# Output projection: two weight tiles in turns over the column chunks, and some element-wise work moved from VectorE to GpSimd

## The chip, the cores and the metric

The kernel runs on one core of a Trainium2 chip. The metric is the device time of one execution in microseconds (us); several runs were made, and their median counts. The engines are TensorE (PE, with weight loads shown apart as PEld), VectorE (DVE), ScalarE (ACT), GpSimd (POOL) and SyncE (SP), which only issues transfers here. Each works through its own list of instructions in order, and instructions of different engines wait for one another by semaphores.

## The reference

Two layers over 16 meta tokens and 1024 frames (T = 1040 columns), model width 1024. Each layer, cut to what matters:

```python
xn = rms_norm(h, attn_norm[i])
gq, gk, gv, gr, glr, fq, fk, fv, ff = jnp.split(xn @ w_in[i], cuts, axis=-1)
o_gla = gla_chunk_causal(...)                       # 4 heads of 128, per chunk of 64 frames
o_gla = rms_norm(o_gla, gla_norm) * jax.nn.silu(gr) # the gate
o_fox = forgetting_attention(...)                   # 8 heads of 64, softmax with a forget bias
o_fox = rms_norm(o_fox, fox_norm)
h = h + jnp.concatenate([o_gla, o_fox], axis=-1) @ w_out[i]
h = h + conv_ffn(rms_norm(h, ffn_norm[i]), w_up[i], conv_w[i], conv_b[i], w_down[i])
```

## The kernel before, in words

Activations lie transposed: 8 feature blocks of 128 partitions, with the T columns along the free dimension. A float32 product is made of three matmuls: each operand is split into a high part (a cast, by ACT) and a low part (operand minus high part, a subtraction), and `mm3` adds high x high (L253), high x low weight (L254) and low x high (L255). Weights arrive by transfers on SP's queue as `raw` tiles; `weights` splits them, ACT writing `hi` (L220) and either GpSimd or DVE writing `lo` (L222):

```python
eng = nc.gpsimd if self.att and not vec else nc.vector
```

`att` is set through the attention part; `vec=True` there sends the subtraction to DVE. A weight tile has 1024 rows, so two `hi` and two `lo` instructions of 128 x 512 each, in rings of buffers that a later tile reuses.

Activations are split by `split`: ACT casts `mh` (L378), DVE subtracts `ml` (L379). The same lines split the transposed probabilities `PT` of the softmax attention.

A layer has `attention`, then the rest of the output projection and the gated feed-forward part. In `attention`, `fox` goes step by step through the softmax attention of 4 pairs of heads; a step has scores `S`, the running maximum `P`/`m` (L706, DVE), an exponential (L714, ACT), transposes (L735, PE), the split into `PT` (L378, L379), and the product with the values, `av` (L753, PE). Between the steps `fox` takes other matmul work from a `Work` queue, so that PE always has something to do. `Work` hands out generators in order; what one is worth in us decides how many blocks a step takes. `plan(p)` fills the queue when pair p begins:

- p = 0, 1, 2: the query, key and value products of the next pair, and the gate product of GLA head p (`gr_products`): `gx` (L658), a sigmoid in several ACT and DVE steps (`ge`, `gy`; L661 to L664, L666, L667), the product of x with its operand, `gog` = x times `og` (L665, DVE), and their product (L669), which is stored in DRAM.
- p = 3: loads of the mix blocks 4, 5, 0, 1, 2 from DRAM into the slots `land` (`h` in the trace), and the gate of GLA head 3, which goes to `land[3]` directly.
- p = 4: the load of block 6, and the first four output tiles (`NSPLIT` = 4 of 8) of the output projection, as queue work. Block 7 is finished only at the end of `fox`, and its contribution is added later.

An output tile goes over three chunks of columns, in the order 784 (256 wide), 400 (384 wide), 0 (400 wide). A unit is one tile and one chunk: 7 feature blocks in the order `KORD` = 4, 5, 0, 1, 2, 3, 6, with three matmuls each, into one PSUM tile `mm` (there are two), then an evacuation by DVE (L1008) that adds the residual. The residual is loaded by POOL transfers (L1003) into the same slots `h`, over the mix block, once that chunk of it is split. The splits of the mix are done by the units of tile 0, as `feed`: the first `FEED` = 2 functions at the unit's start, then one more ahead of each block, and the residual loads last:

```python
for f in feed[:FEED]:
    f()
if not box.get("ahead"):
    box["ahead"] = True
    nxt = box["work"].after(box)
    if nxt is not None and "w" not in nxt:
        nxt["w"] = self.weights(nxt["src"], vec=nxt["vec"])
...
for i, k in enumerate(ks):
    for f in feed[FEED + i:FEED + i + 1]:
        f()
```

The middle part of this asks for the next tile's weights at a tile's first unit. The weights of tile 0 (`ready`) are asked for when `plan(4)` is called.

## Time and profile before

| what | value |
|---|---|
| median of 3 runs | 2539.6 us (2536.96 to 2540.7) |
| profiled execution | 2536.52 us, span 2534.7 us |
| mean granted clock of TensorE | 0.996 |
| PE busy | 2477.9 us (98%) |
| PEld busy | 2415.6 us (95%) |
| DVE busy | 1737.0 us (69%) |
| ACT busy | 1275.9 us (50%) |
| POOL busy | 405.5 us (16%) |

The span is the time from the first to the last recorded instruction; the profiled execution's own time is 1.8 us longer. Busy time is the time in which an engine has an instruction under way. A row of a timeline gives start, duration, engine, line, operation, output and inputs by the program's names, tile sizes, a count, and in brackets the idle time before it with what ended that. The stage of the change lies between 430 and 490 us in layer 0; layer 1 repeats it about 1254 us later.

### The profile page before, as it was taken

What the parts mean: (1) busy time and instruction counts of PE and PEld (TensorE: products, weight loads), DVE (VectorE), ACT (ScalarE), POOL (GpSimd) and SP (SyncE); (2) the same over time, 40 slices, a digit from 0 to 9 for tenths busy, and PEclk for the clock granted to TensorE, in tenths of its full rate; (3) what the DMA queues carried; (4) which work ended last, traced back from release to release, by engine and by line L of the source; (5) the groups of instructions that cost most, each with busy time, mean ns of one, the idle gap of its engine ahead of it and who ended that gap; (6) DMA issues with size and microseconds to landing.
All of it is one profiled execution on the core that took longest, in us unless ns stands there. A gap on an engine that the chain in (4) does not pass through costs nothing.

```text
span 2534.7 us, 48450 instructions
## 1 busy us (share of the span) xinstructions
PE 2477.9 (98%) x19278; PEld 2415.6 (95%) x19278; DVE 1737.0 (69%) x3365; ACT 1275.9 (50%) x2582; POOL 405.5 (16%) x580
## 2 busy tenths in 40 slices
PE   8999999999999999999999999999999999999998
PEld 7989999999999999999999899999999999999997
DVE  7656676769877777853565666777697777787435
ACT  7346666646544445641443466665464444455312
POOL 4033333210000000100200334331100000001002
PEclk9999999999999999999999999999999999999999
DMA  3232134342322224763312222243432222258622
GB/s 122 66 92 68 45 95 130 114 139 72 118 80 80 80 76 135 198 174 103 107 51 68 74 79 70 65 146 106 143 91 91 85 78 80 80 164 184 185 63 77
DMA packets 116211, 258.29 MB, mean 102 GB/s; under 512 B 14624, under 2 KB 31264, under 8 KB 115984
## 3 DMA queue, kind: packets, MB, share of 16 engines
q1 hardware_dynamic: 92832, 181.74, 23.0%
q0 software_dynamic: 22432, 72.71, 10.4%
q8 instruction: 151, 2.47, 0.4%
q10 hardware_dynamic: 720, 0.74, 0.1%
q14 instruction: 76, 0.62, 0.1%
HBM read 174.54 MB, written 67.81 MB: 96 GB/s over the span
## 4 chain that ended last, share of the span: by engine, by line
PE 53%; issue 31%; DVE 8%; DMA 3%; ACT 2%; POOL 2%; SPq 0%; DVEq 0%; POOLq 0%; ACTq 0%
PE mm L253 8%; PE mm L255 7%; PE mm L254 7%; PE down L253 5%; PE down L254 5%; PE down L255 5%; PE av L753 3%; PE tr L735 2%; DVE P L706 2%; PE wo L253 1%; PE wo L255 1%; PE wo L254 1%; PE S L698 1%; DVE cv L1268 1%; PE S L699 1%
## 5 line engine op out<-in xcount | busy, mean ns | idle before, releaser
L253 PE MATMUL up<-x,hi 128*128 128x260 f32 (+1 forms) x2464 | 697.2, 283 | 2.1 <-DVE hg L1275 1.3
L255 PE MATMUL up<-x,hi 128*128 128x260 f32 (+1 forms) x2464 | 695.9, 282 | 2.4 <-DVE x L1097 2.4
L254 PE MATMUL up<-x,lo 128*128 128x260 f32 (+1 forms) x2464 | 696.6, 283 | 0.0
L255 PEld LDWEIGHTS up<-x,hi 128*128 128x128 f32 x2464 | 465.7, 189 | 3.2 <-DVE x L1097 3.2
L253 PEld LDWEIGHTS up<-x,hi 128*128 128x128 f32 x2464 | 464.5, 189 | 3.0 <-DVE hg L1275 1.8
L254 PEld LDWEIGHTS up<-x,lo 128*128 128x128 f32 x2464 | 464.6, 189 | 0.1
L1073 DVE TENSOR_TENSOR lo<-raw,hi 128x512 fp32r<-128x512 f32 x364 | 247.7, 685 | 180.1 <-ACT hi L1072 172.4
L253 PE MATMUL mm<-xh,hi 128*128 128x348 f32 (+4 forms) x1056 | 362.7, 343 | 0.0
L255 PE MATMUL mm<-xl,hi 128*128 128x348 f32 (+4 forms) x1056 | 339.4, 321 | 0.0
L254 PE MATMUL mm<-xh,lo 128*128 128x348 f32 (+4 forms) x1056 | 338.8, 321 | 0.0
L1072 ACT CAST hi<-raw 128x512 fp32r<-128x512 f32 x364 | 224.4, 620 | 141.5 <-PE up L255 84.6
L253 PEld LDWEIGHTS mm<-xh,hi 128*128 128x128 f32 x1056 | 199.5, 189 | 6.3 <-issue 5.3
L254 PEld LDWEIGHTS mm<-xh,lo 128*128 128x128 f32 x1056 | 199.4, 189 | 0.6 <-issue 0.3
L255 PEld LDWEIGHTS mm<-xl,hi 128*128 128x128 f32 x1056 | 198.3, 188 | 0.9 <-issue 0.7
L254 PE MATMUL down<-ah,lo 128*128 128x260 f32 (+1 forms) x704 | 198.3, 282 | 0.8 <-DVE lo L222 0.8
L255 PE MATMUL down<-al,hi 128*128 128x260 f32 (+1 forms) x704 | 198.2, 281 | 0.0
L253 PE MATMUL down<-ah,hi 128*128 128x260 f32 (+1 forms) x704 | 198.0, 281 | 0.0
L220 ACT CAST hi<-raw 128x512 fp32r<-128x512 f32 (+1 forms) x160 | 96.8, 608 | 151.0 <-PE down L255 117.1
L379 DVE TENSOR_TENSOR PT<-tr,PT 116x464 fp32r<-116x464 f32 (+3 forms) x240 | 122.3, 515 | 70.8 <-ACT PT L378 68.9
L714 ACT ACTIVATE P<-P,m 116x924 f32<-116x924 f32 (+4 forms) x144 | 110.5, 767 | 76.4 <-DVE m L706 70.8
L1300 POOL DMA_DIRECT2D actd<-cv x44 | 23.6, 536 | 765.3 <-DVE cv L1299 744.3
L735 PE MATMUL tr<-ident,P 116*116 116x116 f32 x704 | 143.8, 268 | 1.5 <-DVE m L706 1.0
(294 smaller groups left out, 5769.4 us busy)
## 6 DMA issues: line engine op xcount, KB each, us to landing
raw<-in_wm_dram SPq DMA_DIRECT2D x322, 256.0 KB, 2.8
raw<-in_wd_dram SPq DMA_DIRECT2D x64, 256.0 KB, 3.5
actd<-cv POOLq DMA_DIRECT2D x22, 520.0 KB, 3.0
actd<-cv POOLq DMA_DIRECT2D x22, 512.0 KB, 3.1
cb<-cd SPq DMA_DIRECT2D x16, 520.0 KB, 4.3
st<-actd SPq DMA_DIRECT2D x14, 520.0 KB, 5.0
st<-actd SPq DMA_DIRECT2D x14, 512.0 KB, 5.2
kA<-kA SPq DMA_DIRECT2D x24, 260.0 KB, 4.2
```

The lines of the kernel that those rows point to most:

```text
L220: nc.scalar.copy(hi[:, :n, :], raw[:, :n, :])
L253: nc.tensor.matmul(ps, wh, xh[:, c0:c0 + n], start=first, stop=False, skip_group_check=more)
L254: nc.tensor.matmul(ps, wl, xh[:, c0:c0 + n], start=False, stop=False, skip_group_check=more)
L255: nc.tensor.matmul(ps, wh, xl[:, c0:c0 + n], start=False, stop=last, skip_group_check=more)
L379: nc.vector.tensor_tensor(out=lo, in0=src, in1=hi.bitcast(F32), op=ALU.subtract)
L698: nc.tensor.matmul(S[:rows, :n], q["qA"][e][:, qs], q["kA"][e][:, c0:k1], start=True, stop=False)
L706: nc.vector.tensor_tensor_reduce(out=x, in0=S[:rows, :n], in1=cb[:rows, c0:k1], scale=1.0, scalar=(BIG if ci == 0 else m[:rows, ci - 1:ci] ...
L714: nc.scalar.activation(x, x, AF.Exp, scale=-1.0, bias=low, accum_out=(den if nch < 3 else d2[:rows, 0:1]))
L735: nc.tensor.transpose(tr[:w, j, :rows], P[:rows, o:o + w], id_)
L753: nc.tensor.matmul(av[:, a:width], w.rearrange("p a b -> p (a b)"), x, start=(t == 0 and i == 0), stop=(t == last and i == 1))
L1072: nc.scalar.copy(hi[:, :nk, :], src[:, :nk, :])
L1073: nc.vector.tensor_tensor(out=lo[:, :nk, :], in0=src[:, :nk, :], in1=hi[:, :nk, :].bitcast(F32), op=ALU.subtract)
```

## The change

Five things are changed.

1. Tiles 0 and 1 are taken in turns, chunk by chunk: tile 0 chunk 784, tile 1 chunk 784, tile 0 chunk 400, tile 1 chunk 400, tile 0 chunk 0, tile 1 chunk 0 (`add_tiles`). Tiles 2 and 3 follow one after the other, as before.
2. The feed is spread differently. Tile 0's first unit does all splits and residual loads of chunk 784 at its start (`FEED` = 8); the units of tile 1 for chunks 784 and 400 do those of chunk 400 and chunk 0.
3. Tile 1's weights are asked for at tile 0's first unit as before; tile 2's at tile 1's third unit.
4. The low parts of the weights of tiles 0 and 1 are written by GpSimd (`vec` False), two instructions a tile, 8 in the program; the gate's product `gog` is made by GpSimd too, 24 instructions in the program.
5. In the text of the program, two of the three loads of block 6 are moved from plan 4 to plan 3. In POOL's list they stand at the same place as before.

```diff
-FEED = 2
+FEED = 8
...
-        if not box.get("ahead"):
-            box["ahead"] = True
+        box["left"] = box.get("left", box["wait"] + 1) - 1
+        if box["left"] == 0:
             nxt = box["work"].after(box)
             if nxt is not None and "w" not in nxt:
                 nxt["w"] = self.weights(nxt["src"], vec=nxt["vec"])
...
-    def add_tile(self, work, pp, src, xs, chunks, evac, ks=range(KD), w=None, feed=None, vec=False):
+    def add_tile(self, work, pp, src, xs, chunks, evac, ks=range(KD), w=None, vec=False):
+        self.add_tiles(work, pp, [(src, evac, w, {})], xs, chunks, ks, vec)
+
+    def add_tiles(self, work, pp, tiles, xs, chunks, ks, vec):
+        boxes = []
+        for src, evac, w, feed in tiles:
+            box = {"src": src, "work": work, "vec": vec, "wait": len(chunks) - 1 if boxes else 0}
+            if w is not None:
+                box["w"] = w
+            boxes.append(box)
+        work.boxes += boxes
         for j, (c0, n) in enumerate(chunks):
-            work.add(self.unit(pp, box, src, ks, xs, c0, n, evac, (feed or {}).get(j, ())), len(ks) * 3 * mm_us(n))
+            for box, (src, evac, w, feed) in zip(boxes, tiles):
+                work.add(self.unit(pp, box, src, ks, xs, c0, n, evac, feed.get(j, ())), len(ks) * 3 * mm_us(n))
...
-            nc.vector.tensor_tensor(out=og, in0=x, in1=og, op=ALU.mult)
+            nc.gpsimd.tensor_tensor(out=og, in0=x, in1=og, op=ALU.mult)
...
-                        ready = self.weights(self.wm[lyr, M_WO], vec=True)
+                        ready = self.weights(self.wm[lyr, M_WO])
...
-                            first = {} if m else {"w": ready, "feed": {j: split(2 - j) for j in range(3)}}
-                            self.add_tile(w, pp, self.wm[lyr, M_WO + m], mix, chunks[::-1], ev, ks=KORD, vec=True, **first)
+                            feed = {0: split(2)} if m == 0 else {j: split(1 - j) for j in range(2)} if m == 1 else {}
+                            return self.wm[lyr, M_WO + m], ev, None if m else ready, feed
+                        self.add_tiles(w, pp, [out_tile(0), out_tile(1)], mix, chunks[::-1], KORD, False)
+                        for m in range(2, NSPLIT):
+                            self.add_tiles(w, pp, [out_tile(m)], mix, chunks[::-1], KORD, True)
```

Lines below the edited places shift by 8 or 9 in the changed kernel: L379 becomes L387, L753 L761, L665 L673, L1003 L1012, L1008 L1017. In the lists, `h_5777` to `h_5783` are the slots of mix blocks 0 to 6, `mh_6101`/`ml_6102` the split of block 0, 6103/6104 of block 1, 6105/6106 of block 2, 6107/6108 of block 3, 6109/6110 of block 4, 6111/6112 of block 5 and 6113/6114 of block 6. `PT_6140` and `PT_6141` hold the transposed probabilities of one step of the last pair, in several pieces.

DVE's list in layer 0, before, from the first half of `PT_6140` to its second half; the splits of block 6 and of the 384-wide chunk lie between:

```order
L379 TENSOR_TENSOR PT_6140<-tr,PT_6140 116x4x116
L379 TENSOR_TENSOR ml_6114<-h_5783,mh_6113 128x256
L379 TENSOR_TENSOR ml_6110<-h_5781,mh_6109 128x384
L379 TENSOR_TENSOR ml_6112<-h_5782,mh_6111 128x384
L379 TENSOR_TENSOR ml_6104<-h_5778,mh_6103 128x384
L379 TENSOR_TENSOR ml_6106<-h_5779,mh_6105 128x384
L379 TENSOR_TENSOR PT_6141<-tr,PT_6141 116x3x116
L1008 TENSOR_TENSOR h_5777<-mm,h_5777 128x256
L706 ISA P,m<-S,cb 116x460
L706 ISA m 116x1
L379 TENSOR_TENSOR PT_6140<-tr,PT_6140 116x4x116
```

And after, the same stretch:

```order
L387 TENSOR_TENSOR PT_6140<-tr,PT_6140 116x4x116
L387 TENSOR_TENSOR ml_6106<-h_5779,mh_6105 128x384
L387 TENSOR_TENSOR ml_6108<-h_5780,mh_6107 128x384
L387 TENSOR_TENSOR ml_6114<-h_5783,mh_6113 128x384
L387 TENSOR_TENSOR ml_6110<-h_5781,mh_6109 128x400
L387 TENSOR_TENSOR PT_6141<-tr,PT_6141 116x3x116
L1017 TENSOR_TENSOR h_5777<-mm,h_5777 128x256
L714 ISA P,m<-S,cb 116x460
L714 ISA m 116x1
L387 TENSOR_TENSOR ml_6112<-h_5782,mh_6111 128x400
L387 TENSOR_TENSOR PT_6140<-tr,PT_6140 116x4x116
```

The 256-wide split of block 6 has left this stretch and stands some 15 instructions earlier; three more 384-wide splits (blocks 4, 5 and 1) have moved ahead of it too, and three 400-wide splits (block 0 ahead of the stretch, blocks 4 and 5 within it) now come before the second half of `PT_6140`.

PE's list in layer 0, before, ahead of the `av` group that reads `PT_6140`:

```order
L792 MATMUL tr<-ident,ff 128x116 x2
L735 MATMUL tr<-ident,P 116x116 x2
L253 MATMUL mm<-mh_6101,hi 128x384
L254 MATMUL mm<-mh_6101,lo 128x384
L255 MATMUL mm<-ml_6102,hi 128x384
L253 MATMUL mm<-mh_6103,hi 128x384
L254 MATMUL mm<-mh_6103,lo 128x384
L255 MATMUL mm<-ml_6104,hi 128x384
L753 MATMUL av<-PT_6140,V_4635 128x232 x8
```

And after:

```order
L800 MATMUL tr<-ident,ff 128x116 x2
L743 MATMUL tr<-ident,P 116x116 x2
L253 MATMUL mm<-mh_6103,hi 128x256
L254 MATMUL mm<-mh_6103,lo 128x256
L255 MATMUL mm<-ml_6104,hi 128x256
L253 MATMUL mm<-mh_6105,hi 128x256
L254 MATMUL mm<-mh_6105,lo 128x256
L255 MATMUL mm<-ml_6106,hi 128x256
L253 MATMUL mm<-mh_6107,hi 128x256
L254 MATMUL mm<-mh_6107,lo 128x256
L255 MATMUL mm<-ml_6108,hi 128x256
L761 MATMUL av<-PT_6140,V_4635 128x232 x8
```

Where tile 0's second chunk stood, tile 1 now works on the first chunk, whose splits are already there for tile 0.

POOL's list in layer 0, before, around the residual loads of chunk 784:

```order
L987 DMA h_5783<-mixd_96 128x400
L871 TENSOR_TENSOR cb<-cb,mask 116x116
L1003 DMA h_5777<-in_hT_dram 128x256
L1003 DMA h_5778<-in_hT_dram 128x256
L1003 DMA h_5777<-in_hT_dram 128x384
L871 TENSOR_TENSOR cb<-cb,mask 116x116
L1003 DMA h_5779<-in_hT_dram 128x256
L1003 DMA h_5780<-in_hT_dram 128x256
```

And after:

```order
L673 TENSOR_TENSOR gog<-gx,gog 128x348
L1012 DMA h_5777<-in_hT_dram 128x256
L1012 DMA h_5777<-in_hT_dram 128x384
L1012 DMA h_5778<-in_hT_dram 128x256
L1012 DMA h_5777<-in_hT_dram 128x400
L879 TENSOR_TENSOR cb<-cb,mask 116x116
L222 TENSOR_TENSOR lo<-raw,hi 128x512 x2
L673 TENSOR_TENSOR gog<-gx,gog 128x344
L1012 DMA h_5779<-in_hT_dram 128x256
L1012 DMA h_5780<-in_hT_dram 128x256
```

Two gate products and tile 1's two low parts now stand in POOL's list among the residual loads and the mask of the forget bias (L879).

More of the change, by code (lines that the diff above doesn't have):

```diff
@@ L284, in unit @@
         yield 3 * mm_us(n)
-    def add_tile(self, work, pp, src, xs, chunks, evac, ks=range(KD), w=None, feed=None, vec=False):
-        box = {"src": src, "work": work, "vec": vec}
-        if w is not None:
-            box["w"] = w
-        work.boxes.append(box)
+    def add_tile(self, work, pp, src, xs, chunks, evac, ks=range(KD), w=None, vec=False):
[8 more added lines that the diff above has]
+        work.boxes += boxes
         for j, (c0, n) in enumerate(chunks):
-            work.add(self.unit(pp, box, src, ks, xs, c0, n, evac, (feed or {}).get(j, ())), len(ks) * 3 * mm_us(n))
+            for box, (src, evac, w, feed) in zip(boxes, tiles):
+                work.add(self.unit(pp, box, src, ks, xs, c0, n, evac, feed.get(j, ())), len(ks) * 3 * mm_us(n))
     def dense3(self, pp, w, xs, chunks, evac):
@@ L982, in plan @@
                             nc.gpsimd.dma_start(land[k][:, :T], self.mixd[k][:])
+                        for c0, n in CH[:0:-1]:
+                            nc.gpsimd.dma_start(land[6][:, c0:c0 + n], self.mixd[6][:, c0:c0 + n])
                         self.gr_products(lyr, 3, w, ap, pp, nm, land[3])
@@ L985, in plan @@
                         land = box["land"]
-                        for c0, n in reversed(CH):
-                            nc.gpsimd.dma_start(land[6][:, c0:c0 + n], self.mixd[6][:, c0:c0 + n])
+                        nc.gpsimd.dma_start(land[6][:, :CH[1][0]], self.mixd[6][:, :CH[1][0]])
                         for x in nm["x"]:
@@ L1004, in split, with out_tile, ev @@
                             return [lambda k=k: one(k) for k in KORD] + [residual]
-                        for m in range(NSPLIT):
-                            def ev(ps, c0, n, m=m):
+                        def out_tile(m):
+                            def ev(ps, c0, n):
                                 h = hT[m][:, c0:c0 + n]
                                 nc.vector.tensor_tensor(out=h, in0=ps, in1=h, op=ALU.add)
-                            first = {} if m else {"w": ready, "feed": {j: split(2 - j) for j in range(3)}}
-                            self.add_tile(w, pp, self.wm[lyr, M_WO + m], mix, chunks[::-1], ev, ks=KORD, vec=True, **first)
+                            feed = {0: split(2)} if m == 0 else {j: split(1 - j) for j in range(2)} if m == 1 else {}
[3 more added lines that the diff above has]
+                            self.add_tiles(w, pp, [out_tile(m)], mix, chunks[::-1], KORD, True)
                     return w
```

## The prediction

> **What bounds the kernel now.** I read the page's busy line first, then the waits of TensorE (PE), then the stage of the change in order of time, in both layers.

> ```profile
> span 2534.7 us, 48450 instructions
> PE 2477.9 (98%) x19278; PEld 2415.6 (95%) x19278; DVE 1737.0 (69%) x3365; ACT 1275.9 (50%) x2582; POOL 405.5 (16%) x580
> PE mm L255 <- DVE ml L379: 7.2, 4, 3.0
> ```

> PE is busy for 2477.9 of 2534.7 us, so only what makes PE wait, or run at a lower clock, can move the time. The third line is a wait of PE (total us, times, longest): the low x high matmul of the output projection waits four times, 7.2 us in all, for VectorE (DVE) to write a low part `ml`. These four waits are what the change is aimed at. In time they stand here, two per layer:

> ```profile
> 463.26 0.39 PE L255 MATMUL mm<-ml,hi 128*128 128x256 f32 x1 [0.65 <-DVE ml L379]
> 467.25 0.58 PE L255 MATMUL mm<-ml,hi 128*128 128x256 f32 x1 [2.96 <-DVE ml L379]
> 470.14 0.52 PE L253 MATMUL mm<-mh,hi 128*128 128x384 f32 x1
> 472.81 0.34 PE L255 MATMUL mm<-ml,hi 128*128 128x384 f32 x1
> 472.98 1.05 PE L753 MATMUL av<-PT,V 112*128 112x232 f32 x8
> ...
> 1717.08 0.39 PE L255 MATMUL mm<-ml,hi 128*128 128x256 f32 x1 [0.65 <-DVE ml L379]
> 1721.07 0.44 PE L255 MATMUL mm<-ml,hi 128*128 128x256 f32 x1 [2.96 <-DVE ml L379]
> ...
> 1726.21 1.06 PE L753 MATMUL av<-PT,V 112*128 112x232 f32 x8
> 462.00:474.00 12.00, 8.40 (x45) 7.65 (x44) 11.61 (x34) 8.91 (x23) 3.77 (x7) 0.72 0.36 115
> 1716.00:1728.00 12.00, 8.39 (x50) 7.62 (x48) 11.96 (x35) 8.69 (x23) 3.79 (x7) 0.86 0.40 115
> 464.00:465.00 1.00, 0.29 (x3) 0.08 (x1) 1.00 (x5) 1.00 (x4) 0.83 (x2) 1.00 0.79 279
> 465.00:466.00 1.00, 0.00 (x0) 0.00 (x0) 1.00 (x5) 1.00 (x3) 0.29 (x1) 0.58 0.74 229
> ```

> The long wait costs more than its 2.96 us. In the window rows (PE, PEld, DVE, ACT, POOL busy; then PE's granted clock) the clock is 0.72 and 0.86 on average. A clock of one half for 12 x 2 x 0.28 = 6.7 us and 12 x 2 x 0.14 = 3.4 us gives these means, and a 384-column matmul takes 0.52 us in it against 0.34 after. The last two rows put its start at about 465.2, so it ends at 471.9, and PE works in it from 467.25: 4.7 us of work done at half speed, 2.4 us lost. In layer 1 the 3.4 us lie nearly wholly beside work: 1.7 lost. Removed without any replacement, the waits are therefore worth 2 x 3.61 + 2.4 + 1.7 = 11.3 us: 0.45%. That is the most the change can bring here.

> Who is late is shown by DVE:

> ```profile
> 454.30:470.90 16.60, 13.00 (x83) 11.99 (x83) 16.57 (x50) 15.43 (x40) 5.29 (x10) 0.83 0.38 119
> 470.30 0.63 DVE L379 TENSOR_TENSOR PT<-tr,PT 116x464 fp32r<-116x464 f32 x1
> 1724.13 0.63 DVE L379 TENSOR_TENSOR PT<-tr,PT 116x464 fp32r<-116x464 f32 x1
> ```

> DVE works 16.57 of 16.60 us, with no gap that better timing could fill: here the DVE list is the limit. The list ends for PE with the second half of `PT`, 470.93 and 1724.76, which the `av` group needs. Before, PE comes to `av` 2.05 and 1.45 us later than that, and doesn't wait for it.

> **Turns of two tiles.** PE gets six tile-1 blocks of 256 columns (18 matmuls at 0.12) where it had four tile-0 blocks of 384 (12 at 0.17): about 2.1 us of PE work either way. So PE at full clock would reach `av` at 472.98 - 3.61 - 2.4 = 467.0 and 1726.21 - 3.61 - 1.7 = 1720.9. The split of block 6 now stands ahead of the 384 splits; I place it, by the DVE rows in front of it, near 462.2 in layer 0, before PE wants it at 463. That wait goes. What is late next is `PT`: what DVE must do ahead of it changes so:

> ```profile
> 454.34 0.52 DVE L665 TENSOR_TENSOR gog<-gx,gog 128x348 f32<-128x348 f32 x1
> 461.08 0.51 DVE L665 TENSOR_TENSOR gog<-gx,gog 128x344 f32<-128x344 f32 x1
> 461.51 1.29 DVE L222 TENSOR_TENSOR lo<-raw,hi 128x512 fp32r<-128x512 f32 x2
> 470.85 1.01 DVE L379 TENSOR_TENSOR ml<-h,mh 128x384 fp32r<-128x384 f32 x2
> 472.90 2.50 DVE L379 TENSOR_TENSOR ml<-h,mh 128x400 fp32r<-128x400 f32 x5
> ```

> Gone are two gate products and two weight lows, 0.52 + 0.51 + 1.29 = 2.3 us. New ahead of `PT`, since tile 1's units feed them sooner, are two splits of 384 columns (1.01) and three of 400 (3 x 0.50): 2.5 us. So `PT` comes at about 471.1 and 1725.0 instead of 470.9 and 1724.8, and PE, there at 467.0 and 1720.9, waits 4.1 us in each layer. The wait moves from `ml` to `PT`. `av` begins 1.9 and 1.2 us sooner than before, -3.1 in all; a wait of 4.1 brings the half clock too, with up to 1.7 us lost per layer in one 3.4 us stretch, +3.4. Sum of the turns with DVE undisturbed: +0.3, no change.

> **GpSimd beside DVE.** What the moved work costs there, and what it does to DVE, show at other places:

> ```profile
> L222 POOL TENSOR_TENSOR lo<-raw,hi 128x512 fp32r<-128x512 f32 x52 | 66.9, 1292 | 66.5 <-ACT hi L220 66.4
> L621 POOL TENSOR_TENSOR kL<-kt,kA 128x348 fp32r<-128x348 f32 (+1 forms) x24 | 22.3, 929 | 25.6 <-ACT kA L620 22.3 <-issue 3.3
> 268.12 1.29 POOL L222 TENSOR_TENSOR lo<-raw,hi 128x512 fp32r<-128x512 f32 x1
> 268.34 1.46 DVE L667 SCALAR_TENSOR_TENSOR gy<-ge,gy 128x348 f32<-128x348 f32 x1
> 269.83 0.52 DVE L669 SCALAR_TENSOR_TENSOR ge<-gy,gog 128x348 f32<-128x348 f32 x1
> ```

> A weight low takes GpSimd (POOL) 1.29 us against 0.65 on DVE; a product of 348 columns 0.93 against 0.52 (L621 has the gate product's shape). And the two engines don't run side by side: L667, a DVE instruction like L669 and with two operands in SBUF, took 1.46 instead of 0.52, because POOL's low part ran from 268.12 to 269.41 and DVE could begin only then. Between 454 and 466 POOL gets two gate products and two lows: 2 x 0.93 + 2 x 1.29 = 4.4 us. DVE's list there is almost all of that kind (splits, gate steps); only steps reading PSUM went past. The delay has the bounds 0 (every POOL step beside a PSUM reader) and 4.4; I take 3.7, five sixths, since two of the rows there in six or seven read PSUM. Then `av` begins at 471.1 + 3.7 = 474.8 and 1728.7: 1.8 and 2.5 later than before, +4.3 us. The half clock follows the new wait too: between 0 and 1.7 us lost per layer; I take 1.2, as part of it passes inside the wait. Together 4.3 + 2.4 = +6.7. DVE breaks even at a delay of 1.9 us in layer 0 and 1.2 in layer 1.

> [...] With all 4.4 us held off, the sum would be 2 x 0.7 worse, +8.1. [...]

> **The smaller terms.**

> ```profile
> L665 DVE TENSOR_TENSOR gog<-gx,gog 128x348 f32<-128x348 f32 (+1 forms) x24 | 15.2, 634 | 0.0
> 380.00:400.00 20.00, 20.00 (x145) 19.56 (x144) 10.18 (x32) 12.09 (x33) 8.96 (x12) 1.00 0.07 21
> 438.03 0.72 PE L753 MATMUL av<-PT,V 116*128 116x232 f32 x5
> 435.93 0.63 DVE L379 TENSOR_TENSOR PT<-tr,PT 116x464 fp32r<-116x464 f32 x1
> 469.42 0.41 DVE L1008 TENSOR_TENSOR h<-mm,h 128x256 f32<-128x256 f32 x1
> 485.94 0.60 ACT L220 CAST hi<-raw 128x512 fp32r<-128x512 f32 x1
> ```

> - The other gate products (24 less the 2 x 2 above): DVE loses 0.5 us each, POOL gains 0.93. DVE works 10.18 of 20 us there and PE all 20. Cover: DVE's half idle time. I take 0; bounds -1 to +2 us over both layers (a product delayed by POOL's queue holds L669 back, and what DVE has behind it).
> - Tile 0's two lows, near 437: 2.6 us on POOL. `PT` ends at 436.56 and PE takes it at 438.03, so 1.5 us of slack stands against a delay of at most 1.3: 0.
> - On POOL's queue the residual transfers now stand behind a gate product, and the lows ahead of a mask and later transfers. The first evacuation at 469.42 wants its residual, issued near 455.5 in both: 0. A third gate product behind the lows is ready by about 466, its reader near 470 in the delayed list: 0.
> - Tile 2's weights, asked for in tile 1's third unit, can be written only when tile 0's buffers are free, after tile 0's last unit: two casts (0.60) and two DVE lows (0.65), 2.5 us. Cover: tile 1's last unit, 21 x 0.18 = 3.8 us on PE, and fox work beside it. If that cover is gone, up to 1 us per layer. I take 0.

> Sum: +6.7 against this execution's 2536.5 (span 2534.7 and 1.8 around it): 2543.2. The median of the runs, 2539.6, lies 3.1 above this execution; with the same +6.7 it becomes 2546.3.

> **Rivals.**
> 1. Nothing to measure. DVE is held up less, by about 0 to 2 us per layer: `PT` comes at 471 to 473, PE waits at `av`, and the half clock takes what was won: +0.3, 2539.9, between 2536 and 2542.5. For it: PSUM readers go past POOL, and POOL's lows could fall beside them. Against it: the row of 1.46.
> 2. Faster. Both waits vanish: `PT` reaches PE by 467.0, 4 us sooner than DVE's list allows if the splits were as long as before. It would need DVE rows that I count ahead of `PT` to shrink or slip behind it. Price -11.3: 2528.3. Half of it, with the wait but without the half clock (-3.1), 2536.5. Against both: 16.57 of 16.60 us.
> 3. Slower further on: tile 2's conversions late by 1 us per layer and a late gate product, with the delay at its bound: 6.7 + 1.4 + 2 = +10, 2549.7, and up to 2554 with a second half-clock stretch in each layer.

> **How the numbers follow.** About 0.2% (5 us) is what a measurement of this kernel can tell from no change. DVE delayed (forecast): 0.45, of which a tenth stays within 0.2%; rival 1: 0.29; rival 2: 0.21, a quarter of it (its smaller form) within 0.2%; rival 3: 0.05. So slower 0.41 + 0.05 = 0.46, same 0.04 + 0.29 + 0.05 = 0.38, faster 0.16. The forecast's own range is 2540 to 2550, rival 1's 2536 to 2542.5. To leave out no more than 2 in 10 the range goes from 2533, which keeps rival 2's smaller form and leaves out its whole form, to 2553.

> **What would show it.** In the profile after, the waits of L255 on `ml` are gone or under 2 us, and a new one stands in each layer, PE `av` on DVE `PT`, 4 to 8 us. DVE rows of 1 to 2 us where splits took 0.4 to 0.5, each under a POOL product or low, show the delay; DVE's busy time falls by less than the 15.2 + 2 x 2.6 us taken from it. POOL's busy time rises by 24 x 0.93 + 8 x 1.29 = 32.6 us to 438. The granted clock drops to a half behind the new wait. The forecast is wrong if splits keep their 0.4 to 0.5 us beside POOL, if `PT` ends before 471 in layer 0, or if PE waits for something other than `PT`.

## The result, and the profile after

The changed kernel takes 2556.1 us (median of 4, 2554.5 to 2556.6) against 2539.2 for the kernel before in the same comparison: 16.9 us slower, ratio 1.006 with a 95% interval of 1.0048 to 1.0071. The sign was forecast, the size was not: 2546.3 with a range up to 2553.

The page of the changed kernel, its busy line, and the three rows of PE's waits (total us, times, longest) that matter in the stages of the change:

```profile
span 2554.8 us, 48492 instructions
PE 2488.7 (97%) x19278; PEld 2424.2 (95%) x19278; DVE 1747.2 (68%) x3333; ACT 1278.3 (50%) x2582; POOL 438.7 (17%) x612
PE S L706 <- DVE m L714: 14.0, 8, 2.4
PE mm L255 <- DVE ml L387: 3.4, 2, 1.7
PE av L761 <- DVE PT L387: 1.7, 4, 0.4
```

Two things stand in it. DVE has 32 instructions less, which took 20.4 us before (24 products, 15.2 us, and 8 low parts of 0.65), and is yet busy for 10 us more: it is held. And PE's long wait is now neither `ml` (7.2 before) nor `PT`, but the scores `S` (4.4 before), which wait for the maximum step `m` of DVE. PE is also busy 10.8 us longer with the same matmuls: the granted clock is 0.991 to 0.992 in the four runs of the changed kernel, and 0.993 to 0.998 in those of the kernel before (all but one, which at a clock of 0.644 took 4144 us).

Where the time went is read from the same `av` matmul in both traces, its start after minus its start before:

| us in the kernel before | after minus before |
|---|---|
| 300, behind the gate stage of head 0 | +2.0 |
| 380, head 1 | +5.3 |
| 446.5, head 2 and tile 0's low parts | +8.8 |
| 500, behind the last stage | +8.7 |
| 1500, end of layer 0 | +8.6 |
| 1550, 1630, 1700: heads 0, 1, 2 of layer 1 | +11.8, +15.1, +18.3 |
| 1760, behind the last stage | +18.8 |

The last stage, where the forecast put all of the loss, adds nothing in layer 0 and 0.5 us in layer 1. Each gate stage of heads 0 to 2, where it put nothing, costs 2 to 3.5 us. So the change reaches further than the stretch from 430 to 490 us named at the start: the 18 products of heads 0 to 2 stand from 256 us on. In the stage of head 0, before:

```profile
272.83 0.15 DVE L777 TENSOR_TENSOR fv<-fv,fd 112x2 f32<-112x2 f32 x1
274.87 0.34 DVE L661 TENSOR_SCALAR ge<-gx 128x348 f32<-128x348 f32 x1 [1.24 <-DMA mixd<-ge]
275.72 0.63 DVE L706 CUSTOM_DVE_ANT_0 P<-S,cb 116x460 f32<-116x460 f32 x1
276.42 0.31 PE L735 MATMUL tr<-ident,P 116*116 116x116 f32 x1 [0.61 <-DVE m L706]
277.99 0.46 PE L698 MATMUL S<-kA,qA 128*116 128x460 f32 x1 [1.26 <-DVE m L706]
```

And after (lines are 8 higher):

```profile
271.15 2.54 POOL L222 TENSOR_TENSOR lo<-raw,hi 128x512 fp32r<-128x512 f32 x2
273.65 0.92 POOL L673 TENSOR_TENSOR gog<-gx,gog 128x348 f32<-128x348 f32 x1
271.67 2.93 DVE L785 TENSOR_TENSOR fv<-fv,fd 112x2 f32<-112x2 f32 x1
276.03 0.63 DVE L714 CUSTOM_DVE_ANT_0 P<-S,cb 116x460 f32<-116x460 f32 x1
276.73 0.31 PE L743 MATMUL tr<-ident,P 116*116 116x116 f32 x1 [0.97 <-DVE m L714]
278.49 0.46 PE L706 MATMUL S<-kA,qA 128*116 128x460 f32 x1 [1.45 <-DVE m L714]
281.28 0.49 PE L253 MATMUL mm<-xh,hi 128*128 128x344 f32 x1
```

L785 (L777 before) multiplies two numbers per partition, 0.15 us. After, it takes 2.93: it begins while POOL runs two weight low parts and a gate product one behind the other, 271.15 to 274.57, and ends only behind them. The slack that DVE had there, 1.24 us waiting for a transfer, is used up; the maximum steps come later, and `S` with them, 278.49 against 277.99. PE was waiting there before as well, so the stage had no cover on PE. In this execution the longer waits are followed by the half clock (the last row: 0.49 us for a matmul that takes 0.32 at full clock); the two low parts run back to back here, where before they stood apart, at 268.12 and 271.22, with two transfer issues of POOL between them. The rows by stage (PE, PEld, DVE, ACT, POOL busy, then PE's clock), before and after:

```profile
275.00:285.00 10.00, 7.92 (x54) 6.92 (x53) 6.96 (x21) 7.21 (x17) 3.11 (x5) 1.00 0.14 44
355.00:370.00 15.00, 13.83 (x101) 13.08 (x100) 10.83 (x31) 9.32 (x22) 5.20 (x8) 1.00 0.23 77
440.00:455.00 15.00, 14.66 (x103) 13.77 (x102) 12.56 (x33) 9.76 (x24) 3.68 (x7) 1.00 0.35 110
```

```profile
275.00:285.00 10.00, 7.36 (x39) 6.51 (x38) 6.80 (x21) 7.21 (x17) 2.70 (x5) 0.83 0.17 58
355.00:370.00 15.00, 12.35 (x77) 11.40 (x77) 11.77 (x28) 9.12 (x24) 6.86 (x10) 0.89 0.30 91
440.00:455.00 15.00, 12.86 (x79) 11.79 (x78) 12.39 (x31) 8.74 (x24) 6.43 (x9) 0.89 0.31 92
```

Each gate stage has a new stretch of half clock: 10 x 2 x 0.17 = 3.4 us, about 1.7 us of work lost. Six of them are 10 us; PE's time without a matmul in these three stages rises from 4.4 to 8.3 us in layer 0 and from 4.2 to 8.0 in layer 1, 8 us in both. Together 18 of the 18.8.

### The profile page after: what moved, and what is told of

Its sections match the earlier page's. It is cut to its first block, busy times and chain, and to the rows that moved or that the text cites. A ratio compares the mean times of both kernels' runs of the same rounds, so it can differ in the third digit from the quotient of the medians.

```text
span 2554.8 us, 48492 instructions
## 1 busy us (share of the span) xinstructions
PE 2488.7 (97%) x19278; PEld 2424.2 (95%) x19278; DVE 1747.2 (68%) x3333; ACT 1278.3 (50%) x2582; POOL 438.7 (17%) x612
## 4 chain that ended last, share of the span: by engine, by line
PE 80%; DVE 10%; issue 5%; ACT 2%; DMA 2%; POOL 0%; DVEq 0%; SPq 0%; ACTq 0%; POOLq 0%
PE up L253 9%; PE up L254 9%; PE up L255 9%; PE mm L253 8%; PE mm L254 8%; PE mm L255 8%; PE down L253 5%; PE down L254 5%; PE down L255 5%; PE av L761 3%; PE tr L743 2%; PE wo L253 1%; PE wo L255 1%; PE wo L254 1%; DVE P L714 1%
## 5 line engine op out<-in xcount | busy, mean ns | idle before, releaser
L253 PE MATMUL up<-x,hi 128*128 128x260 f32 (+1 forms) x2464 | 697.3, 283 | 2.2 <-DVE hg L1287 1.4
L255 PE MATMUL up<-x,hi 128*128 128x260 f32 (+1 forms) x2464 | 695.9, 282 | 2.3 <-DVE x L1109 2.3
L255 PEld LDWEIGHTS up<-x,hi 128*128 128x128 f32 x2464 | 465.7, 189 | 3.2 <-DVE x L1109 3.2
L253 PEld LDWEIGHTS up<-x,hi 128*128 128x128 f32 x2464 | 464.5, 189 | 3.2 <-DVE hg L1287 1.8
L253 PE MATMUL mm<-xh,hi 128*128 128x348 f32 (+4 forms) x1056 | 366.2, 347 | 0.0
L255 PE MATMUL mm<-xl,hi 128*128 128x348 f32 (+4 forms) x1056 | 341.8, 324 | 0.0
L253 PEld LDWEIGHTS mm<-xh,hi 128*128 128x128 f32 x1056 | 202.1, 191 | 6.3 <-issue 5.3
L255 PEld LDWEIGHTS mm<-xl,hi 128*128 128x128 f32 x1056 | 200.9, 190 | 1.0 <-issue 0.7
L255 PE MATMUL down<-al,hi 128*128 128x260 f32 (+1 forms) x704 | 198.2, 281 | 0.0
L253 PE MATMUL down<-ah,hi 128*128 128x260 f32 (+1 forms) x704 | 198.0, 281 | 0.0
L387 DVE TENSOR_TENSOR PT<-tr,PT 116x464 fp32r<-116x464 f32 (+3 forms) x240 | 122.6, 516 | 75.1 <-ACT PT L386 72.4
L220 ACT CAST hi<-raw 128x512 fp32r<-128x512 f32 (+1 forms) x160 | 96.8, 609 | 152.7 <-PE down L255 117.1
L1067 DVE TENSOR_TENSOR raw<-raw,raw 128x512 f32<-128x512 f32 x198 | 130.1, 691 | 24.8 <-DMA raw<-in_wd_dram 21.2
```

What stands on the lines that cost most here:

```text
L220: nc.scalar.copy(hi[:, :n, :], raw[:, :n, :])
L253: nc.tensor.matmul(ps, wh, xh[:, c0:c0 + n], start=first, stop=False, skip_group_check=more)
L255: nc.tensor.matmul(ps, wh, xl[:, c0:c0 + n], start=False, stop=last, skip_group_check=more)
L387: nc.vector.tensor_tensor(out=lo, in0=src, in1=hi.bitcast(F32), op=ALU.subtract)
L1067: nc.vector.tensor_tensor(out=q[out][:, :nk, :], in0=q[a][:, :nk, :], in1=q[b][:, :nk, :], op=op)
```

## The experiments

Theory A, from these traces: the product on GpSimd is paid in the gate stages of heads 0 to 2, where a run of POOL instructions holds DVE. Theory B, the forecast's: it is paid in the last stage. All runs below were timed against the kernel before on the same chip; its median was 2540.1, 2539.5 and 2539.9 us in the three groups.

**The product back on DVE.**

```diff
-nc.gpsimd.tensor_tensor(out=og, in0=x, in1=og, op=ALU.mult)
+nc.vector.tensor_tensor(out=og, in0=x, in1=og, op=ALU.mult)
```

> The changed kernel with the gate's product back on DVE (24 instructions); turns, feed and the low parts on GpSimd stay. Theory A: the loss lies in the gate stages of heads 0 to 2, where POOL's run of two weight lows and a product holds a tiny DVE instruction for 2.9 us and PE's clock then falls by half; so the time falls by 15 to 19 us against the changed kernel, to 2537 to 2541 us, and the half-clock stretches near 280, 366 and 449 us vanish. Theory B (the forecast's): the loss lies in the last stage, where GpSimd's work delays PT; then two of four products less there give back at most 3 us per layer: 2550 or more.

2541.3 us, ratio 1.0008 (0.9999 to 1.0017). 14.8 us of the 16.9 are the product's.

**Only the product, on the kernel before.**

```diff
-nc.vector.tensor_tensor(out=og, in0=x, in1=og, op=ALU.mult)
+nc.gpsimd.tensor_tensor(out=og, in0=x, in1=og, op=ALU.mult)
```

> The kernel before with one edit: the gate's product on GpSimd. Theory A: this one edit makes nearly the whole loss, 14 to 18 us: 2553 to 2557 us, with DVE instructions of 2.9 us in the gate stages of heads 0 to 2. Theory B: there is idle DVE time to hide it in those stages, so 0 to 4 us: 2539 to 2543. A third possibility, that only the product together with tile 0's lows makes the third head's stage late: 11 us, 2550.

2552.0 us, 1.0053 (1.0039 to 1.0066): +11.9, far from B, and between A and the third possibility. The hold is there without any other part of the change (its row stands with the short product, below). The trace decides for the third: the stages of heads 0 and 1 are late here too, but in that of head 2 PE waits 0.42 us for `S`, and the `av` behind it is 0.1 us earlier in layer 0 and 0.3 later in layer 1 within the stage, against 3.5 and 3.2 later in the changed kernel, where tile 0's low parts stand ahead of the product. With the product alone, and in the changed kernel:

```profile
446.90 0.47 PE L698 MATMUL S<-kA,qA 128*116 128x460 f32 x1 [0.42 <-DVE m L706]
```

```profile
449.37 0.47 PE L706 MATMUL S<-kA,qA 128*116 128x460 f32 x1 [1.65 <-DVE m L714]
```

**The product on GpSimd for head 3 alone.**

```diff
-nc.gpsimd.tensor_tensor(...)
+(nc.vector if dst is None else nc.gpsimd).tensor_tensor(...)
```

> The changed kernel with the product on DVE for heads 0 to 2 (18 instructions) and on GpSimd for head 3 alone (6). Theory A: like the run with all products on DVE, 2537 to 2541 us, since the last stage of the changed kernel was as long as before. Theory B: the last stage keeps the loss, 2548 or more. The difference to the run with all products on DVE is the price of the product in the last stage: by A within 2 us.

2545.5 us, 1.0019 (1.001 to 1.0029). A's range was missed: the six products of head 3 cost 4.2 us, where A said under 2, and B has a part of the truth. Heads 0 to 2 make the difference to the changed kernel, 10.6 us. PE's waits in the last stage of layer 0, with all products on DVE and with head 3's on GpSimd:

```profile
467.41 0.39 PE L255 MATMUL mm<-ml,hi 128*128 128x256 f32 x1 [1.40 <-DVE ml L387]
470.28 0.73 PE L706 MATMUL S<-kA,qA 128*116 128x460 f32 x1 [1.98 <-DVE m L714]
476.17 1.04 PE L761 MATMUL av<-PT,V 112*128 112x232 f32 x7 [0.79 <-DVE PT L387]
```

```profile
462.11 1.05 PE L761 MATMUL av<-PT,V 112*128 112x232 f32 x7 [0.85 <-DVE PT L387]
468.80 0.39 PE L255 MATMUL mm<-ml,hi 128*128 128x256 f32 x1 [1.66 <-DVE ml L387]
472.14 0.73 PE L706 MATMUL S<-kA,qA 128*116 128x460 f32 x1 [2.49 <-DVE m L714]
```

These waits are 4.2 and 5.0 us: they show the direction, and not the whole of the price.

**The turns alone** (the product and the low parts of tiles 0 and 1 on DVE).

```diff
-ready = self.weights(self.wm[lyr, M_WO])
+ready = self.weights(self.wm[lyr, M_WO], vec=True)
-self.add_tiles(w, pp, [out_tile(0), out_tile(1)], mix, chunks[::-1], KORD, False)
+self.add_tiles(w, pp, [out_tile(0), out_tile(1)], mix, chunks[::-1], KORD, True)
```

> The changed kernel with the product and the low parts of tiles 0 and 1 back on DVE: the turns and the feed alone. Theory A: PE's wait moves from ml to PT or S in the last stage and nothing else moves; DVE's list there is 2.3 us longer than in the changed kernel, with no GpSimd work beside it: 2538 to 2544 us. Rival C (the low parts on GpSimd are a loss of their own, in the last stage and near 440 us): the turns alone gain, 2530 to 2536.

2536.8 us, 0.9989 (0.9979 to 0.9999): a small gain, under A's lower end and at the edge of rival C's range. The low parts on GpSimd therefore cost 4.5 us (2541.3 less 2536.8). In the last stage of layer 0 the two `ml` waits, 3.61 us, have become one of 1.90 for `S` and two at `av`, 3.44 us in all (2.8 in layer 1), and the half clock in layer 0's last stage has shrunk from 6.8 to 3.4 us:

```profile
469.34 0.47 PE L706 MATMUL S<-kA,qA 128*116 128x460 f32 x1 [1.90 <-DVE m L714]
473.22 0.37 PE L761 MATMUL av<-PT,V 112*128 112x232 f32 x1 [0.36 <-ACT PT L386]
474.78 1.05 PE L761 MATMUL av<-PT,V 112*128 112x232 f32 x7 [1.18 <-DVE PT L387]
```

**Tile 0's low parts back on DVE, tile 1's on GpSimd** (from the run with the product on DVE).

```diff
-ready = self.weights(self.wm[lyr, M_WO])
+ready = self.weights(self.wm[lyr, M_WO], vec=True)
```

> The changed kernel with the product on DVE (2541.3 us) and tile 0's two low parts back on DVE as well; tile 1's stay on GpSimd. Theory A, from the lags of the traces: tile 0's lows cost 1.5 us a layer near 440 us, so 2538 to 2539. If all of the 4.5 us between that run and the turns alone (2536.8) lie with tile 1's lows beside the splits: 2541. If all lie with tile 0's: 2537.

2539.9 us, 1.0004 (0.9995 to 1.0012). By the medians tile 0's low parts cost 1.5 us and tile 1's 3.1, and 0.8 and 3.7 when each run is set against the kernel before of its own group; runs of one kernel spread over 4 us and more, so this split is rough.

**The run of POOL instructions broken** (the product on GpSimd on the kernel before, and the fox key weights' low parts on DVE).

```diff
-self.add_tile(work, pp, self.wm[lyr, m], xs, CH_FOX, ev)
+self.add_tile(work, pp, self.wm[lyr, m], xs, CH_FOX, ev, vec=m == M_FK + p)
```

> The kernel before with the product on GpSimd, as in the run of the product alone (2552.0 us), and one edit more: the low parts of each fox key weight tile go to DVE, so that the two weight lows no longer stand back to back in front of a gate product in POOL's list. Theory A (a run of GpSimd instructions holds DVE for its whole length): the 2.9 us hold of the tiny DVE instruction falls to under 1 us in the stages of heads 0 to 2, and 6 to 10 us come back: 2542 to 2546. Rival D (the product is late for its reader, whatever stands ahead of it, or DVE's list is simply short of time): 2550 or more.

2536.0 us, 0.9991 (0.9982 to 1.0): 16 us come back where A said 6 to 10. D is out, but A is short of something: these low parts cost time even before (the run with them alone on DVE, below, shows it).

**The product of heads 0 to 2 cut to 4 columns** (the rest isn't multiplied; the order of POOL's list is the changed kernel's).

```diff
-nc.gpsimd.tensor_tensor(out=og, in0=x, in1=og, op=ALU.mult)
+m = n if dst is not None else 4
+nc.gpsimd.tensor_tensor(out=og[:, :m], in0=x[:, :m], in1=og[:, :m], op=ALU.mult)
```

> The changed kernel (2556.1 us) with the gate product of heads 0 to 2 on GpSimd cut to 4 of its columns; the other columns are not multiplied. POOL's list keeps the order of the changed kernel, with both lows back to back. Theory A: the hold of the tiny DVE instruction falls from 2.9 to about 2.0 us, which the wait of DVE for a transfer right behind it (1.2 us in the kernel before) hides: 2545 to 2548, near the run without these products on GpSimd (2545.5). Rival E (the loss comes from the new order of POOL's list, not from the product's time): 2553 or more.

2543.3 us, 1.0016 (1.0007 to 1.0025), 2 us below A's range; E is out. The time of the product counts, not its place. The tiny instruction shows it, with its shortest, median and longest duration (ns). In the kernel before and in the changed one:

```profile
L777 DVE TENSOR_TENSOR fv<-fv,fd x40: 147/161/608, 210.3 to 1768.1; 116x4 f32<-116x4 f32 x32, 112x2 f32<-112x2 f32 x8
```

```profile
L785 DVE TENSOR_TENSOR fv<-fv,fd x40: 151/163/2935, 210.2 to 1786.9; 116x4 f32<-116x4 f32 x32, 112x2 f32<-112x2 f32 x8
```

With the product alone, with the short product and with the run broken:

```profile
L777 DVE TENSOR_TENSOR fv<-fv,fd x40: 149/161/2939, 211.8 to 1780.4; 116x4 f32<-116x4 f32 x32, 112x2 f32<-112x2 f32 x8
```

```profile
L786 DVE TENSOR_TENSOR fv<-fv,fd x40: 150/164/2048, 213.0 to 1778.1; 116x4 f32<-116x4 f32 x32, 112x2 f32<-112x2 f32 x8
```

```profile
L777 DVE TENSOR_TENSOR fv<-fv,fd x40: 149/162/899, 210.5 to 1771.0; 116x4 f32<-116x4 f32 x32, 112x2 f32<-112x2 f32 x8
```

The longest is what is left of POOL's run: 2.9 us with two low parts and a product, 2.0 with the product cut, 0.9 with a product alone. DVE's 1.24 us of slack can hide the last.

**The early feed alone**, on the kernel before.

```diff
-FEED = 2
+FEED = 8
```

> The kernel before with FEED = 8 alone: no turns, nothing on GpSimd. DVE's list in the last stage is then the same as that of the turns alone. If the gain of that run (3.3 us) comes from the earlier split of block 6: 2535 to 2538. If the turns are needed for it, because tile 0's 384-wide blocks come before their splits: PE waits for ml of the second chunk and the time is 2539 to 2543.

2537.9 us, 0.9995 (0.9986 to 1.0004). It can't be told from the kernel before, nor from the turns alone; whether the turns add anything to the early split of block 6 stays open. Its trace says which wait the early feed itself removes: PE's waits for `ml` are 1.6 us in all, where they were 7.2, and those for `S` 9.9, where they were 4.4.

**The key weights' low parts on DVE, without the product on GpSimd**, and **the same with the turns** (the edit of the broken run, on the kernel before and on the turns alone).

> The kernel before with the low parts of the fox key weights on DVE and nothing else. The run with the product on GpSimd and these lows on DVE took 2536.0 us. If that time is owed to the lows alone, 2534 to 2538 here; if the product on GpSimd is a gain of its own once nothing stands ahead of it, 2538 to 2541.

> The turns alone (2536.8 us), with the low parts of the fox key weights moved from GpSimd to DVE as well; the product stays on DVE. If these lows already held DVE in the kernel before, where L667 and L665 took 1.46 and 1.26 us under them, the half clock near 280 us becomes rarer and 1 to 4 us come off: 2533 to 2536. If DVE's extra 0.65 us each eats it: 2536 to 2539.

2533.5 us, 0.9974 (0.9964 to 0.9984), and 2530.2 us, 0.9962 (0.995 to 0.9975). The first lies below its range: the low parts alone gain 6.4 us, and the product on GpSimd costs 2.5 us even with nothing ahead of it (2.9 against the kernel before of each group). The second beats the kernel before by 9.7 us and the changed one by 26. In the stage of head 0 PE's wait for `S` falls from 1.26 to 0.42 us, and no half clock follows:

```profile
274.97 0.31 PE L743 MATMUL tr<-ident,P 116*116 116x116 f32 x1 [0.18 <-DVE m L714]
275.71 0.47 PE L706 MATMUL S<-kA,qA 128*116 128x460 f32 x1 [0.42 <-DVE m L714]
```

**The same with the product on GpSimd.**

> As the run before it, with the gate's product on GpSimd: turns, product on GpSimd, all low parts of this stage and of the key weights on DVE. In the stages of heads 0 to 2 the product then costs nothing (from the run with the broken run of instructions). In the last stage two products stand alone on GpSimd beside the splits: if they cost what the difference of 4.2 us between the split product and all products on DVE says, 2537 to 2541; if that price came from product and lows standing one behind the other there, 2533 to 2536.

2540.4 us, 1.0007 (0.9998 to 1.0015): 10.2 us more than with the product on DVE, the first of the two cases expected, at its upper end. PE's waits with the product on DVE and on GpSimd:

```profile
PE S L706 <- DVE m L714: 5.3, 6, 1.9
PE av L761 <- DVE PT L387: 3.6, 7, 1.2
PE av L761 <- ACT PT L386: 0.4, 1, 0.4
```

```profile
PE S L706 <- DVE m L714: 8.1, 8, 1.4
PE av L761 <- DVE PT L387: 6.7, 6, 1.6
PE av L761 <- ACT PT L386: 2.7, 3, 1.2
```

Here the product costs 8.2 us of waits in these rows, and without the turns only 2.5 us of time. In the order without turns PE still waits for `ml` in the last stage, and that wait shrinks with the product on GpSimd, from 7.2 to 4.2 us in all. The half clock of that stage shrinks too, from 6.8 us in each layer to 3.4 in layer 1 alone; the granted clock is 0.995 or 0.996 in the eight runs with the product on DVE and 0.996 to 0.999 in the eleven with it on GpSimd. That it is this which pays for the product there is read from the two traces and was not tested by itself.

## Why the prediction was wrong

The medians give each part of the change a price, one part put on after another: the turns -3.3, tile 1's low parts +3.1, tile 0's +1.5, the product of head 3 +4.2, that of heads 0 to 2 +10.6. (Each run set against the kernel before of its own group: -3.3, +3.7, +0.8, +4.2, +11.5, which add up to the 16.9.) These prices hold for this order. The sign came out as forecast, but most of the loss lies where the forecast put nothing, so the sign is in good part luck. The forecast's sum and these:

- **The other gate products: taken as 0, bounds -1 to +2; measured +10.6.** This is the step that failed, and it alone puts the time outside the range. The cover named was "DVE's half idle time", a mean over 20 us (10.18 of 20, from 380 to 400). No gate product stands in that window: before, those of head 1 begin between 339.7 and 354.9, those of head 2 between 422.5 and 436.7. Where the stages are, DVE was busy for 76, 85 and 88%:

```profile
264.00:288.00 24.00, 21.92 (x156) 20.54 (x155) 18.12 (x51) 15.67 (x39) 8.77 (x12) 1.00 0.19 60
345.00:367.00 22.00, 20.83 (x149) 19.66 (x148) 18.68 (x56) 15.37 (x39) 8.12 (x12) 1.00 0.25 80
432.00:452.00 20.00, 19.66 (x141) 18.58 (x140) 17.60 (x52) 13.19 (x32) 5.06 (x10) 1.00 0.34 105
```

  And what counts lies at one place of 7 us: POOL's list in the changed kernel has two low parts and the product in one run there (at head 2 one of tile 0's low parts and the product), and DVE's list has behind them the steps on which `S` depends. The hold of DVE under GpSimd's work was priced for the last stage and not for this one. The view that would have shown it for heads 0 and 1 stood in the waits of PE before: 0.61 and 1.26 us for `m` at 276 to 278, and 0.96 at 360, places with no slack. At head 2 PE did not wait for `m` before.
- **The half clock was counted in the last stage alone.** Six of the new stretches are in the gate stages, some 10 us.
- **The last stage: forecast +6.7, measured +4.0** by the medians (turns, tile 1's low parts, head 3's product, put on while the other products were on DVE). In the changed kernel's own trace this stage adds only 0.4 us in both layers together, as the table shows; why the same parts cost less behind the late gate stages stays open. The delay of DVE was rightly sized, 3.7 taken. In layer 0 the rows are these:

```profile
462.23 1.96 DVE L387 TENSOR_TENSOR ml<-h,mh 128x256 fp32r<-128x256 f32 x3
469.02 0.51 DVE L666 TENSOR_TENSOR gx<-mm,r 128x344 f32<-128x344 f32 x1
469.25 2.79 POOL L222 TENSOR_TENSOR lo<-raw,hi 128x512 fp32r<-128x512 f32 x2 [2.72 <-ACT hi L220]
469.44 1.12 DVE L785 TENSOR_TENSOR fv<-fv,fd 116x4 f32<-116x4 f32 x1
470.82 1.41 DVE L669 TENSOR_SCALAR ge<-gx 128x344 f32<-128x344 f32 x1
472.15 1.46 DVE L387 TENSOR_TENSOR ml<-h,mh 128x256 fp32r<-128x256 f32 x2
```

  L666, which reads PSUM, runs its usual 0.51 under the low part. L785, L669 and the splits are held by 1.0, 1.1 and 0.7 us, and those at 462.23 by 0.7 under the first product: 3.5 us. The new wait was placed wrongly. PE stops at `S`, ahead of `av`:

```profile
473.34 0.39 PE L255 MATMUL mm<-ml,hi 128*128 128x256 f32 x1 [1.67 <-DVE ml L387]
476.69 0.73 PE L706 MATMUL S<-kA,qA 128*116 128x460 f32 x1 [2.43 <-DVE m L714]
482.61 1.04 PE L761 MATMUL av<-PT,V 112*128 112x232 f32 x7 [0.42 <-DVE PT L387]
```

  Their 4.5 us are near the 3.61 of before, with the same 6.8 us of half clock in layer 0. Against the `av` group ahead of the stage, this one (without its first matmul, which doesn't wait) is 0.9 us later in layer 0 and 1.5 in layer 1, where 1.8 and 2.5 were forecast; by 500 us this has come back in layer 0, and by 1760 a third of it in layer 1.
- **Tile 0's low parts: taken as 0, measured about +1.5** with the product on DVE. The slack of 1.5 us at 438 was read at `av`; the low parts land in the same run of POOL as the third head's product, and with that product on GpSimd the stage of head 2 is 3.5 and 3.2 us late, where the product alone left it as it was. So a part of the 10.6 is owed to the two together.
- **Right:** the `ml` waits fell from 7.2 to 3.4 us (under 2 us each), POOL's busy time rose to 438.7 (438 forecast), and DVE is held: its busy time was to fall by less than the 20.4 us taken from it, and rose by 10.2. The turns without GpSimd came to -3.3 us, where +0.3 was forecast.

## What to carry to other kernels

Work moved to GpSimd is not hidden by DVE's mean idle time (here 9.8 of 20 us, and the products of heads 0 to 2 still cost 10.6 us): look up what else stands in POOL's list just there, add up the run, and ask what DVE instruction meets it and who waits behind that one. A place where TensorE already waits has no cover, and there some tenths of a us of delay can bring a stretch of half clock that costs more than they do: in head 0's stage PE's two waits grew from 1.87 to 2.42 us, and 3.4 us of half clock followed, about 1.7 us of work. Whether it came depended on where the grid described below lay in that execution. The gain here lay the other way: taking GpSimd's low parts away from such a place gave 6.4 us, and with the turns 9.7.
